# Seven block products in place of eight for 48 of the 160 weight tiles of a hybrid decoder layer

## The chip, the cores and the metric

The kernel runs on one core of one Trainium2 chip. The metric is the device time of one execution in microseconds; the median of three runs is what is compared. The page and the trace come from one further execution, recorded by the hardware profiler.

## The reference, cut to what matters

One layer for 544 tokens (512 of a prompt, 32 of a decode batch) at width 1024, all in fp32:

```python
z = x @ w_in                                     # bg cg hc q k v o ig fg gc gm
conv, new_buf = short_conv(cg * hc, conv_buf, conv_w)
y_conv = (bg * conv) @ w_conv_out
h, C, n, m = mlstm_chunkwise(q, k, v, log i, log f, ...)
y_m = (head_norm(h) * mh_g * sigmoid(o)) @ w_m_out
merged = sigmoid(gc) * y_conv + sigmoid(gm) * y_m
x1 = layer_norm(ALPHA * x + merged @ w_o)
hid = square(relu(x1 @ w_ff1))                   # 4096 wide
x2 = layer_norm(ALPHA * x1 + hid @ w_ff2)
```

The products that the change speaks of are `x` times the columns of gc and gm (both gates), the two branch outputs `w_conv_out` and `w_m_out`, and, of the second MLP product, the parts of two of the four 1024-wide chunks of `hid`.

## The kernel before

Activations lie transposed: 128 partitions, 8 row blocks of the 1024 features, 544 tokens along the free dimension. The weights are 160 tiles of 128 output features each, in the order k, q, o, v, conv (cg, hc, bg for each of 8 feature blocks), w_conv_out, gc, (gm and w_m_out alternating), w_o, and four chunks of 8 first and 8 second MLP tiles.

fp32 accuracy comes from three products of halves. A weight tile is loaded from DRAM (`wload`, L105, SP's queue, 512 KB), ScalarE casts it to a rounded half `wh` (L140) and VectorE takes the rest, `wl = raw - wh` (L141). `mm` (L151) then issues, for each of 8 row blocks, wh times a_h, wh times a_l, wl times a_h, each for two halves of 272 tokens: 48 matmuls to a tile, into one PSUM tile of two banks. The buffers `wr`, `wh`, `wl` are three deep each. Activations are split in the same way (`split`, L555 and L556).

Four PSUM banks serve the products (two tiles of two banks, or four of one where `half`, the loop over one half of the tokens, runs), four more serve everything else (`aux`).

After the gates and k, q, o, v come the prompt's mLSTM and the decode mLSTM, which loads and writes 32 state tiles of 258 KB; the convolution's products run between them. Then, in program order: the convolution output is split into slots 2 and 3, the 8 w_conv_out tiles give y1, the 8 gc tiles give a sigmoid that GpSimd multiplies into y1 (L570), and for each of 8 feature blocks the gm tile, the w_m_out tile and the merge follow, whose result is split again. w_o runs half by half with its weights resident (`resident`, L610 and L611), the first norm of one half beside the other half's products; the MLP's first tiles run the same way, with the resident weights' remainders taken on GpSimd there. Then come whole tiles up to the last 8, which run half by half again beside the second norm.

Every engine's instruction order is fixed before the run: the framework orders them by priority (program order, unless `high_priority` raises a stretch) against its own model of the durations, and a tile takes a buffer of its pool as soon as that model says that one is free. All weight loads go through SP's queue in that order.

Of the kernel before, what the change touches and what calls it, by code (L numbers as in the profile page):

```python
# [31 lines left out]
# columns of the packed small operands  # L32
# [10 lines left out]
# order of the weight tiles  # L43
W_K, W_Q, W_O, W_V, W_CONV, W_YC, W_GC, W_GM, W_OUT, W_FF = 0, 8, 16, 24, 32, 56, 64, 72, 88, 96


@with_exitstack
def tile_hybrid(ctx: ExitStack, tc: tile.TileContext, xT, wt, wg, pk, caug,
# [29 lines left out]
    def slot(i, pl=slots):  # L78
        return pl.tile([P, KT, NT], F32, name=f"slot{i}", tag=f"slot{i}")
# [87 lines left out]
    mstk = ExitStack()          # what the mLSTM keeps to its end  # L167
# [12 lines left out]
    pstk = ExitStack()          # what only the prompt's mLSTM needs  # L180
# [69 lines left out]
    # rows that matmuls spread over the partitions, in exact halves: c, w_inter of the prompt  # L250
# [31 lines left out]
    # per-token columns: a, w_inter, ws, exp(-m)  # L282
# [14 lines left out]
    # decay weights of S, transposed (s on partitions)  # L297
# [17 lines left out]
    qT, so = slot(3), slot(4)  # L315
# [9 lines left out]
    for ft in range(KT):  # L325
        h, d0 = ft // 2, (ft % 2) * P
        ps = mtile(W_V + ft, xh, xl)
        vt = tmp.tile([P, NT], F32, name=f"vt{ft}", tag="cg")
# [5 lines left out]
        vr = tmp.tile([P, 4, NS], F32, name=f"vr{ft}", tag="vr")  # L334
# [118 lines left out]
    # P: rows hi, hi, lo, lo, against v's rows hi, lo, hi, lo  # L453
# [7 lines left out]
    # k*ws: rows hi, hi, lo, lo of the 32 tokens  # L461
# [13 lines left out]
    # q*w_inter, hi and lo, each batch's columns alone  # L475
# [43 lines left out]
    bc = slot(5)  # L519
# [53 lines left out]
    late = pool("late")  # L573
    hh, hl = slot(6, late), slot(7, late)
    for ft in range(KT):
        split(so[:, ft], hh, hl, ft)
    mh, ml = slot(2), slot(3)
    for ft in range(KT):
        ps = mtile(W_GM + 2 * ft, xh, xl)
        sg = tmp.tile([P, NT], F32, name=f"sgm{ft}", tag="cg")  # L580
        nc.scalar.activation(hview(sg), pv(ps), AF.Sigmoid)
        ps = mtile(W_GM + 2 * ft + 1, hh, hl)
        nc.vector.tensor_tensor(hview(sg), pv(ps), hview(sg), op=ALU.mult)
        nc.vector.tensor_tensor(sg, y1[:, ft], sg, op=ALU.add)
        split(sg, mh, ml, ft)

# [33 lines left out]
    def lt(nm, tag, bufs=2, n=HN):  # L620
        return lnp.tile([P, HW], F32, name=nm, tag=tag, bufs=bufs)[:, :n]
# [306 lines left out]
```

## Time and profile before

| what | value |
|---|---|
| median of three runs | 1099.6 us (1097.28 to 1100.43) |
| the profiled execution, first to last instruction | 1099.7 us |
| its mean granted TensorE clock | 0.988 of full speed |
| PE busy (matmul) | 1071.2 us, 97% |
| DVE busy | 535.5 us, 49% |
| ACT busy | 347.9 us, 32% |
| POOL busy | 143.0 us, 13% |
| matmuls | 8351, of them 7680 by L151 |
| moved by DMA | 110.37 MB, 100 GB/s on average |

PE is TensorE's matmul row, PEld its weight loads, DVE VectorE, ACT ScalarE, POOL GpSimd, SP the engine from whose queue most transfers are issued. An engine's busy time says nothing about what it waited for; a duration in the trace holds also the time in which an instruction that had started could not go on.

### The profile page before, as it was taken

How to read it: one execution, taken by the hardware profiler on the slowest of the kernel's cores; microseconds unless marked ns; L12 is line 12 of the kernel's file. 1: busy time of each engine (PE TensorE's matmuls, PEld its weight loads, DVE VectorE, ACT ScalarE, POOL GpSimd, SP SyncE). 2: the span in 40 equal slices, each digit the busy share in tenths (PEclk: the TensorE clock that was granted, in tenths of full speed). 3: DMA queues.
4: the chain of work that ended last, by engine and by line, in shares of the span. 5: the costliest groups of instructions: out<-in, count | busy, mean ns of one | idle time of the engine just before them, and what ended most of it. 6: DMA issues, size and time to landing. Idle time of an engine off the chain costs nothing.

```text
span 1099.7 us, 19420 instructions
## 1 busy us (share of the span) xinstructions
PE 1071.2 (97%) x8351; PEld 1060.0 (96%) x8351; DVE 535.5 (49%) x882; ACT 347.9 (32%) x516; POOL 143.0 (13%) x161
## 2 busy tenths in 40 slices
PE   8999999999999989999999999899999999999994
PEld 8999999999999989999999999899999999999994
DVE  5533223365578778522143359742344234334576
ACT  6431222232234334213222225441233133123432
POOL 1000230000017563003200004200000000000033
PEclk9999999999999999999999999899999999999997
DMA  6222222211136775222222342112222222222201
GB/s 233 98 78 77 97 83 90 77 45 53 40 135 203 241 209 162 95 96 77 97 79 95 123 171 96 58 58 75 80 97 77 97 81 93 94 80 97 96 23 60
DMA packets 34349, 110.37 MB, mean 100 GB/s; under 512 B 3928, under 2 KB 6232, under 8 KB 34008
## 3 DMA queue, kind: packets, MB, share of 16 engines
q1 hardware_dynamic: 31704, 100.69, 28.2%
q0 software_dynamic: 2560, 8.46, 2.0%
q8 instruction: 65, 1.06, 0.4%
q14 instruction: 20, 0.16, 0.1%
HBM read 97.32 MB, written 11.81 MB: 99 GB/s over the span
## 4 chain that ended last, share of the span: by engine, by line
PE 90%; DVE 4%; DMA 3%; ACT 1%; issue 1%; POOL 0%; SPq 0%; DVEq 0%; POOLq 0%; ACTq 0%
PE ps L151 82%; DMA cr<-in_caug_dram 1%; DMA out_cs_dram<-cr 1%; PE u L419 1%; PE pq L496 1%; PE n L405 1%; DVE slot L733 1%; PE S L386 1%; PE n L402 1%; DMA wr<-in_wt_dram 1%; DVE bq L743 1%; DVE slot L671 0%; PE us L507 0%; PE ht L367 0%; PE kt L412 0%
## 5 line engine op out<-in xcount | busy, mean ns | idle before, releaser
L151 PE MATMUL ps<-slot,wh 128*128 128x272 f32 (+1 forms) x4640 | 801.2, 290 | 3.9 <-DVE slot L671 1.8
L151 PEld LDWEIGHTS ps<-slot,wh 128*128 128x128 f32 x4640 | 669.0, 189 | 7.0 <-DVE slot L671 2.5
L151 PE MATMUL ps<-slot,wl 128*128 128x272 f32 (+1 forms) x2320 | 498.2, 289 | 0.0
L151 PEld LDWEIGHTS ps<-slot,wl 128*128 128x128 f32 x2320 | 371.6, 189 | 0.7
L140 ACT CAST wh<-wr 128x1024 fp32r<-128x1024 f32 x145 | 152.1, 1050 | 501.1 <-PE ps L151 437.3
L141 DVE TENSOR_TENSOR wl<-wr,wh 128x1024 fp32r<-128x1024 f32 x142 | 174.1, 1226 | 205.8 <-ACT wh L140 201.7
L151 PE MATMUL ps<-slot,res 128*128 128x272 f32 (+2 forms) x720 | 92.8, 289 | 0.0
L151 PEld LDWEIGHTS ps<-slot,res 128*128 128x128 f32 x720 | 91.3, 188 | 0.3
L726 POOL TENSOR_TENSOR slot<-slot,bc 128x288 f32<-128x288 f32 (+1 forms) x6 | 5.8, 992 | 360.2 <-ACT bc L724 360.2
L810 DVE TENSOR_TENSOR slot<-ps,slot 128x544 f32<-128x544 f32 x16 | 11.6, 725 | 59.3 <-PE ps L151 59.3
L503 POOL TENSOR_SCALAR km<-kk,pkt 128x256 fp32r<-128x256 f32 x32 | 37.3, 1168 | 14.6 <-PE us L507 7.8
L492 ACT CAST ch<-cr 128x516 fp32r<-128x516 f32 x32 | 19.9, 623 | 49.6 <-DMA cr<-in_caug_dram 28.7
L785 ACT CAST slot<-rl 128x544 fp32r<-128x544 f32 (+1 forms) x40 | 22.2, 556 | 37.2 <-DVE rl L784 37.1
L786 DVE TENSOR_TENSOR slot<-rl,slot 128x544 fp32r<-128x544 f32 (+1 forms) x40 | 24.4, 611 | 19.6 <-ACT slot L785 19.4
L509 DVE SCALAR_TENSOR_TENSOR cr<-cr,dec,us 128x258 f32<-128x258 f32 x64 | 29.3, 475 | 3.3 <-PE us L507 3.1
L324 POOL TENSOR_SCALAR slot<-slot,pkt 128x544 f32<-128x544 f32 x8 | 16.8, 2096 | 107.9 <-ACT slot L323 107.9
L493 DVE TENSOR_TENSOR cl<-cr,ch 128x516 fp32r<-128x516 f32 x32 | 22.1, 697 | 17.6 <-ACT ch L492 17.5
L784 DVE TENSOR_TENSOR rl<-rl 128x544 f32<-128x544 f32 (+1 forms) x40 | 24.3, 607 | 11.8 <-ACT rl L783 11.8
L570 POOL TENSOR_TENSOR slot<-slot,sgc 128x544 f32<-128x544 f32 x8 | 14.5, 1809 | 88.1 <-ACT sgc L569 88.1
L783 ACT ACTIVATE rl<-ps 128x544 f32<-128x544 f32 (+1 forms) x40 | 21.2, 529 | 14.3 <-PE ps L151 14.3
L496 PE MATMUL pq<-ch,qm 128*64 128x258 f32 x64 | 18.3, 292 | 5.9 <-ACT wh L140 3.2
L141 POOL TENSOR_TENSOR wl<-wr,wh 128x1024 fp32r<-128x1024 f32 x3 | 7.3, 2423 | 124.9 <-PE am L645 121.2
(258 smaller groups left out, 715.2 us busy)
## 6 DMA issues: line engine op xcount, KB each, us to landing
wr<-in_wt_dram SPq DMA_DIRECT2D x160, 512.0 KB, 3.5
cr<-in_caug_dram SPq DMA_DIRECT2D x32, 258.0 KB, 3.9
out_cs_dram<-cr POOLq DMA_DIRECT2D x32, 258.0 KB, 3.9
slot<-in_xT_dram SPq DMA_DIRECT2D x8, 272.0 KB, 6.3
slot<-in_xT_dram SPq DMA_DIRECT2D x1, 2176.0 KB, 8.5
out_yT_dram<-slot SPq DMA_DIRECT2D x4, 288.0 KB, 2.4
out_cp_dram<-state SPq DMA_DIRECT2D x1, 1028.0 KB
out_yT_dram<-slot SPq DMA_DIRECT2D x4, 256.0 KB, 2.3
```

The costliest lines, as they stand in the source:

```text
L140: nc.scalar.copy(hi, raw)
L141: eng.tensor_tensor(lo, raw, hi.bitcast(F32), op=ALU.subtract)
L151: nc.tensor.matmul(ps[:m, hf, :cs.stop - cs.start], w[:, ws], r(a[:, kt, cs]), start=(kt == 0 and w is wh and a is ah), stop=(kt == KT - 1 ...
L492: nc.scalar.copy(r(chh), cr)
L493: nc.vector.tensor_tensor(r(cl), cr, chh, op=ALU.subtract)
L496: nc.tensor.matmul(pq[:2 * NS, :VW], r(qm[:, dt, bb * 2 * NS:(bb + 1) * 2 * NS]), r(part[:, dt]), start=(bb == 0 and dt == 0 and part is chh),
L503: nc.gpsimd.tensor_scalar(r(km), kk[:, 2 * h:2 * h + 2].rearrange("p a d -> p (a d)"), col("bsel")[:, bb:bb + 1], None, op0=ALU.mult)
L509: nc.vector.scalar_tensor_tensor(cr[:, dt], cr[:, dt], dec[:, h, 4 + bb:5 + bb], pu[:, :VW], op0=ALU.mult, op1=ALU.add)
L783: nc.scalar.activation(view(rl_), src, AF.Relu)
L784: nc.vector.tensor_tensor(rl_, rl_, rl_, op=ALU.mult)
L785: nc.scalar.copy(r(dh[:, ft, cs]), rl_)
L786: nc.vector.tensor_tensor(r(dl[:, ft, cs]), rl_, dh[:, ft, cs], op=ALU.subtract)
```

## The change

Per pair of output feature blocks (j and j+4) the product of a 2 by 2 block weight with a 2 by 2 block activation (feature halves by token halves) is formed from 7 block products in place of 8, in the Winograd form. A block product is 4 row blocks times 3 products of halves, 12 matmuls of 272 columns. A pair has 84 matmuls where two tiles have 96. There are 24 pairs: 4 for gc, 4 for w_conv_out, 4 for gm, 4 for w_m_out, and 4 for each of chunks 1 and 2 of the second MLP product.

```diff
+    class Opset:
+        def sums(self, nm, j, z, eng):
+            t = ztile(f"tt{nm}").rearrange("p a (b n) -> p (a b) n", b=2)
+            x1_ = z[:, 0].rearrange("p (a n) -> p a n", a=2)
+            eng.tensor_tensor(t[:, 0:2], z[:, :, HN:], x1_, op=ALU.subtract)
+            eng.tensor_tensor(t[:, 2], z[:, 1, HN:], t[:, 0], op=ALU.subtract)
+            eng.tensor_tensor(t[:, 3], z[:, 1, :HN], t[:, 2], op=ALU.subtract)
+            split(self.t[0][:, j], self.t[1][:, j], t)
+        def take(self, nm, j, z, eng):
+            ph, pl = self.p
+            split(ph[:, j, 0:2], pl[:, j, 0:2], z[:, :, :HN])
+            split(ph[:, j, 2], pl[:, j, 2], z[:, 1, HN:])
+            self.sums(nm, j, z, eng)
...
+    def halves(nm, src, tag=""):
...
+        nc.scalar.copy(hi, src)
+        nc.vector.tensor_tensor(lo, src, hi.bitcast(F32), op=ALU.subtract)
+    def wpair(i0, i1):
+        a, b = wload(i0), wload(i1)
...
+        a1, a2, b1, b2_ = a[:, :H], a[:, H:], b[:, :H], b[:, H:]
+        tt = nc.gpsimd.tensor_tensor
+        tt(s1, b1, b2_, op=ALU.add)
+        tt(s2, s1, a1, op=ALU.subtract)
+        tt(b1, a1, b1, op=ALU.subtract)
+        tt(s4, a2, s2, op=ALU.subtract)
+        g1 = halves(f"{i0}a", a)
+        g2 = halves(f"{i0}b", s[:, :2 * H])
+        g3 = halves(f"{i0}c", b)
+        g4 = halves(f"{i0}d", s4, "d")
...
+    def spair(i0, i1, X, ev):
+        w = wpair(i0, i1)
+        A = mmt(f"A{nm}")
+        prod(A, w["W11"], X, "X11", True)
+        p1 = ev.part("p1", nm, A[:, :HN])
+        step()
+        F = mmt(f"F{nm}")
+        prod(F, w["W12"], X, "X21", True)
+        ev.add("c11", F[:, :HN], p1)
+        step()
+        prod(A, w["S2"], X, "T2", False)
+        q = ev.part("q", nm, A[:, :HN])
+        D = mmt(f"D{nm}")
+        prod(D, w["S1"], X, "T1", True)
+        prod(A, w["S3"], X, "T3", False)
+        w_ = ev.part("w", nm, A[:, :HN])
+        ev.add("c22", D[:, :HN], w_)
+        def t0():
+            prod(A, w["W22"], X, "T4", False)
+            ev.c21(A[:, :HN])
+        def t1():
+            prod(D, w["S4"], X, "X22", False)
+            ev.add("c12", D[:, :HN], q)
+            ev.done()
+        tail.extend((t0, t1))
...
+    class Evac:
+        def part(self, tag, nm, ps):
+            t = sp.tile([P, HN], F32, name=f"{tag}{nm}", tag=tag, bufs=2 if tag == "q" else 1)
+            nc.scalar.copy(t, ps)
+            return t
+        def add(self, k, ps, t):
+            nc.vector.tensor_tensor(self.block(k), ps, t, op=ALU.add)
+        def c21(self, ps):
+            nc.scalar.copy(self.block("c21"), ps)
...
+    class Added(Evac):
+        def onto(self, k, ps):
+            nc.vector.tensor_tensor(self.block(k), ps, self.block(k), op=ALU.add)
...
+    B = o2set()
+    for j in range(KH):
+        z_ = ztile(f"bz{j}")
+        nc.sync.dma_start(z_, prows(bD, j))
+        B.take(f"b{j}", j, z_, nc.gpsimd)
...
+        def gc(j=j, gz=gz):
+            nc.scalar.activation(gz, gz, AF.Sigmoid)
+            nc.sync.dma_start(prows(cD, j), gz)
+
+        spair(W_GC + j, W_GC + j + KH, X, Evac(gz, gc))
...
+        def gated(j=j, yz=yz):
+            sg = ztile(f"sgc{j}")
+            nc.sync.dma_start(sg, prows(cD, j))
+            nc.vector.tensor_tensor(yz, yz, sg, op=ALU.mult)
+            nc.sync.dma_start(prows(yD, j), yz)
+
+        spair(W_YC + j, W_YC + j + KH, B, Evac(yz, gated))
+    flush()
+    H = o2set()
...
+        def merge(j=j, mz=mz):
+            sg = ztile(f"sgm{j}")
+            nc.sync.dma_start(sg, prows(gD, j))
+            y1 = ztile(f"y1{j}")
+            nc.sync.dma_start(y1, prows(yD, j))
+            nc.vector.tensor_tensor(mz, mz, sg, op=ALU.mult)
+            nc.vector.tensor_tensor(mz, mz, y1, op=ALU.add)
+            split(prows(mh, j), prows(ml, j), mz)
+
+        spair(W_GM + 2 * j + 1, W_GM + 2 * (j + KH) + 1, H, Evac(mz, merge))
+    flush()
...
+    for ck in (1, 2):
+        ahead_()
+        for j in range(1, KH):
+            hidden(ck, j)()
+        ahead_ = hidden(ck + 1, 0)
+        for j in range(KH):
+            i0 = W_FF + 16 * ck + 8
+            spair(i0 + j, i0 + j + KH, D[ck], Added(prows(x1, j)))
+        flush()
```

`wpair` forms four sums of weight halves on GpSimd (512 columns each) and splits seven half tiles (ScalarE casts, VectorE subtracts). `step` runs the two block products that a pair leaves over (t0 and t1) inside the next pair, `flush` runs them at once. One sum of activations, T1 to T4 of a pair of row blocks, is three GpSimd subtractions of 544, 272 and 272 columns. The sums of x are formed during the convolution, whose feature blocks now run in the order 0, 4, 1, 5, 2, 6, 3, 7; for them x is read from DRAM again.

The convolution's result, the mLSTM's, both sigmoids and y1 are written to DRAM (`bD`, `hD`, `cD`, `gD`, `yD`, 2.2 MB each) and read back in pairs of row blocks. After `flush`, the mLSTM's operands H are formed while gm, which takes only x, runs; the convolution's operands B are formed while gc runs. `hidden(ck, j)` makes first MLP tiles j and j+4, and its `put` takes them into the operands of chunk ck. The pools change too: `zz` (three buffers of two row blocks), `sp` (one buffer each of the weight sums `ws`, the outputs `zb`, the last weight half), `o2` (one set of operands). The products of the changed stages use four single banks, `mtile1` replaces `mtile` after the merge, the first chunk's activation takes one buffer `zb` where it had two, the hidden values of chunks 1 to 3 are squared by ScalarE, and `x1` is read in eight transfers in place of one.

## Rows read from the trace of the kernel before

**Rows 1.** Page, part 1: busy time and share of the span by engine.

```profile
PE 1071.2 (97%) x8351; PEld 1060.0 (96%) x8351; DVE 535.5 (49%) x882; ACT 347.9 (32%) x516; POOL 143.0 (13%) x161
```

**Rows 2.** Windows: length, busy us (instructions) by engine, granted clock, DMA share, GB/s.

```profile
215.00:445.00 230.00, 224.14 (x1700) 218.47 (x1699) 162.89 (x369) 79.37 (x131) 67.86 (x94) 0.99 0.42 134
541.00:640.00 99.00, 99.00 (x791) 99.00 (x790) 37.95 (x42) 30.56 (x36) 0.00 (x0) 1.00 0.34 118
640.00:700.00 60.00, 55.72 (x409) 54.22 (x408) 46.87 (x66) 22.20 (x35) 20.00 (x8) 0.94 0.32 106
```

**Rows 3.** Waits: engine and line, releaser, us in total, times, longest.

```profile
ACT wh L140 <- PE ps L151: 437.3, 109, 16.5
```

**Rows 4.** Timeline of the gc stage, VectorE and GpSimd: start, us, instruction.

```profile
498.31 1.36 POOL L570 TENSOR_TENSOR slot<-slot,sgc 128x544 f32<-128x544 f32 x1 [60.10 <-ACT sgc L569]
502.32 1.23 DVE L141 TENSOR_TENSOR wl<-wr,wh 128x1024 fp32r<-128x1024 f32 x1 [4.77 <-ACT wh L140]
502.88 1.88 POOL L570 TENSOR_TENSOR slot<-slot,sgc 128x544 f32<-128x544 f32 x1 [3.21 <-ACT sgc L569]
508.32 1.23 DVE L141 TENSOR_TENSOR wl<-wr,wh 128x1024 fp32r<-128x1024 f32 x1 [4.77 <-ACT wh L140]
```

**Rows 5.** Lines by form: instructions, busy us, mean ns of one, idle before.

```profile
L141 DVE TENSOR_TENSOR wl<-wr,wh 128x1024 fp32r<-128x1024 f32 x142 | 174.1, 1226 | 205.8 <-ACT wh L140 201.7
L556 DVE TENSOR_TENSOR slot<-slot,slot 128x544 fp32r<-128x544 f32 x16 | 10.9, 719 | 0.7 <-ACT slot L555 0.7
L784 DVE TENSOR_TENSOR rl<-rl 128x272 f32<-128x272 f32 x16 | 7.0, 439 | 11.8 <-ACT rl L783 11.8
L689 DVE SCALAR_TENSOR_TENSOR slot<-slot,ps 128x272 f32<-128x272 f32 x16 | 6.8, 432 | 10.5 <-PE ps L151 10.5
L759 POOL TENSOR_TENSOR slot<-slot,bms 128x512 f32<-128x512 f32 x2 | 2.5, 1266 | 7.1 <-ACT bms L756 7.1
L742 POOL TENSOR_TENSOR bs<-bs,slot 128x256 f32<-128x256 f32 x3 | 2.3, 782 | 0.2
L140 ACT CAST wh<-wr 128x1024 fp32r<-128x1024 f32 x145 | 152.1, 1050 | 501.1 <-PE ps L151 437.3
L783 ACT ACTIVATE rl<-ps 128x272 f32<-128x272 f32 x16 | 6.3, 397 | 14.3 <-PE ps L151 14.3
```

**Rows 6.** Timeline of the first norm, VectorE and GpSimd, 662 to 668 us.

```profile
661.98 2.41 POOL L141 TENSOR_TENSOR wl<-wr,wh 128x1024 fp32r<-128x1024 f32 x1 [121.22 <-PE am L645]
662.02 2.62 DVE L648 TENSOR_TENSOR slot<-slot,am 128x544 f32<-128x544 f32 x4 [0.65 <-PE am L645]
665.46 2.40 POOL L141 TENSOR_TENSOR wl<-wr,wh 128x1024 fp32r<-128x1024 f32 x1 [1.07 <-ACT wh L140]
665.65 2.50 DVE L691 TENSOR_TENSOR as<-slot 128x272 f32<-128x272 f32 x1
```

**Rows 7.** Timeline of the same engines where three GpSimd subtractions follow each other.

```profile
685.94 7.71 POOL L611 TENSOR_TENSOR res<-wr,res 128x1024 fp32r<-128x1024 f32 x3 [5.92 <-issue]
686.39 2.54 DVE L671 TENSOR_TENSOR slot<-slot,slot 128x544 fp32r<-128x544 f32 x1 [0.16 <-ACT slot L670]
688.86 2.58 DVE L691 TENSOR_TENSOR as<-as,slot 128x272 f32<-128x272 f32 x1
691.36 2.88 DVE L671 TENSOR_TENSOR slot<-slot,slot 128x544 fp32r<-128x544 f32 x1
```

**Rows 8.** Windows of 3 us over and after that stretch, columns as in rows 2.

```profile
688.00:691.00 3.00, 0.69 (x4) 0.42 (x3) 3.00 (x2) 0.80 (x1) 3.00 (x2) 1.00 0.47 162
691.00:694.00 3.00, 2.19 (x8) 1.73 (x8) 3.00 (x2) 0.00 (x0) 2.66 (x2) 0.66 0.56 184
694.00:697.00 3.00, 2.71 (x12) 2.71 (x13) 3.00 (x6) 1.60 (x3) 0.00 (x0) 0.50 0.51 183
697.00:700.00 3.00, 3.00 (x19) 3.00 (x19) 2.60 (x6) 1.57 (x4) 0.00 (x0) 0.70 0.00 0
```

**Rows 9.** DMA issues between 300 and 430 us: count, KB each, median us to landing.

```profile
wr<-in_wt_dram SPq DMA_DIRECT2D x15, 512.0 KB, 4.3
```

More of the change, by code (lines that the diff above doesn't have):

```diff
@@ L13 @@
 PSUM = bass.MemoryType.PSUM
+DRAM = bass.MemoryType.DRAM
 P = 128
@@ L23 @@
 KT = 8
+KH = KT // 2
 NH = 4
@@ L573, in tile_hybrid @@
[L573 to L585, printed above, removed]
@@ new lines, in prod, with step @@
+    def prod(ps, w, X, which, start):
+        wh, wl = w
+        for kt in range(KH):
+            ws = slice(kt * P, (kt + 1) * P)
+            for n, (w_, lo) in enumerate(((wh, 0), (wh, 1), (wl, 0))):
+                nc.tensor.matmul(ps[:, :HN], w_[:, ws], r(X.get(which, kt, lo)),
+                                 start=(start and kt == 0 and n == 0),
+                                 stop=(kt == KH - 1 and n == 2), skip_group_check=True)
+    tail = []
+    def step():
+        if tail:
+            tail.pop(0)()
@@ L613, in resident, with rplaces @@
         return out
+    def rplaces(t):
+        return sum((spots(slot(k, (P, KT * NT), F32R)) for k in (2, 3)), []) + ppspot(t)
     def half(i, ft, w, ah, al, cs, mid=None):
@@ new lines, in tile_hybrid @@
+    res = resident(W_FF, rplaces(pp), nc.gpsimd)
+    dh, dl = slot(0), slot(1)
+    for hf in range(2):
+        for ft in range(KT):
+            run(ft)
+            ps = half(W_FF + ft, ft, res[ft], xh1, xl1, hv[hf])
+            rl = sp.tile([P, 2, NT], F32, name=f"rl{ft}_{hf}", tag="zb")[:, 0, :HN]
+            nc.scalar.activation(rl, ps, AF.Relu)
+            nc.vector.tensor_tensor(rl, rl, rl, op=ALU.mult)
+            split(dh[:, ft, hv[hf]], dl[:, ft, hv[hf]], rl)
+    ahead_ = hidden(1, 0)
@@ new lines, in tile_hybrid, with sums @@
+    dh, dl = slot(0), slot(1)
+    ahead_()
+    for j in range(1, KH):
+        hidden(3, j)()
+    i0 = W_FF + 56
+    lt2 = Small([o2.tile([P, 15, HW], F32, name="ln2", tag="tl")])
+    res = resident(i0, rplaces(o2.tile([P, 2 * KH * 3 * HN], F32, name="pp2", tag="pp")))
+    for hf in range(2):
+        st = {}
+        def sums(hf=hf, st=st):
+            st["ps"] = aux(f"bm{hf}"), aux(f"bv{hf}")
+            for ps, t0 in zip(st["ps"], (st["s"], st["q"])):
+                nc.tensor.matmul(ps[:, :hv2[hf].stop - hv2[hf].start], onek, t0,
+                                 start=True, stop=False)
+        for ft in range(KT):
+            run(ft)
+            ps = half(i0 + ft, ft, res[ft], dh, dl, hv2[hf], sums if ft == 7 else None)
+            with tc.high_priority(offset=300):
+                norm2_part(lt2, hf, ft, ps, st)
+        if hf == 0:
+            later[1] = lambda st=st: norm2(lt2, 0, st)
+        else:
+            norm2(lt2, 1, st)
```

301 lines of the change are left out of this document (188 added, 113 removed).

## The prediction, on record before the run

> **What bounds the kernel now.** The page's busy shares come first: PE is at work for 1071 of 1099.7 us and no other engine for more than half [rows 1]. The stage windows say where that holds: between 541 and 640 us, in the gm, w_m_out and w_o tiles, PE has not a microsecond free and full clock, while VectorE works 38 of 99 us and GpSimd not at all [rows 2]. The waits agree: ScalarE waits 437 us for PE to give up a weight buffer [rows 3]. So TensorE's instruction stream is the path, and the weights' preparation is hidden. One tile's period is read from the subtraction that splits each: 502.32 to 508.32, 6.00 us [rows 4], for 48 matmuls, 0.125 us each. Fewer matmuls are worth that much, as long as the work per tile elsewhere stays hidden. That is the question, since this change buys 12.5% of TensorE's work in a stage with much more work on VectorE and GpSimd.
>
> **What is removed.** A pair takes 84 x 0.125 = 10.5 us of PE in place of 12.0. Over 24 pairs: 36.0 us, the most that it can give. 16 pairs lie in the gates and branch outputs (192 us now, 168 us of PE after), 8 in the MLP (96 to 84).
>
> **What is added to VectorE and GpSimd.** From the durations by form [rows 5]: a VectorE subtraction of 1024 columns is 1.23 us, of 544 0.72, of 272 0.44; along that slope 512 columns are 0.69 and 1088 are 1.29 (estimates). GpSimd takes 1.27 us for 512, 0.78 for 256, hence some 0.80 for 272, and 1.36 for 544 undisturbed [rows 4].
> - Weights of a pair: four GpSimd sums, 5.1 us, and three and a half VectorE remainders, 3 x 1.23 + 0.69 = 4.4 us (two, 2.5 us, now).
> - Operand sums of one pair of row blocks: GpSimd 1.36 + 2 x 0.80 = 3.0, VectorE 0.72 + 0.44 + 1.29 = 2.5; 5.4 us, 21.6 for the four pairs of B, and again of H.
> - VectorE besides: multiplying by the gate 1.29 for each w_conv_out pair, merge and split 3 x 1.29 = 3.9 for each w_m_out pair, three sums out of PSUM at 0.43 each.
>
> By each engine alone all of this fits under 10.5 us a pair. But do VectorE and GpSimd run at once? A 272-column VectorE add with both inputs in SBUF started at 665.65, took 2.50 us and ended 0.29 us after the GpSimd subtraction that had started at 665.46 [rows 6]; it needs 0.44 otherwise [rows 5]. The other way round, GpSimd's multiply at 502.88 took 1.88 us, and it ended 1.21 us after VectorE's subtraction did [rows 4]. With three GpSimd subtractions in a row, three VectorE adds took 2.54, 2.58 and 2.88 us [rows 7]. VectorE operations that read PSUM are free of this: four at 662.02 took 0.66 us each under a running GpSimd one [rows 6]. So all sums on GpSimd and all remainders on VectorE take turns, and their durations add up. The Trainium skill, "SBUF — State Buffer", section "SBUF: two separate sides", says the same of a VectorE operation with two SBUF inputs against a GpSimd operation that reads SBUF: whichever starts first has the shared port for its whole instruction, and the other is fully blocked. The rows above agree. By that rule alone, without the packing below, the section that follows would be 17 us longer than before.
>
> **The gates and branch outputs.** Taking turns, a pair costs 5.1 + 4.4 = 9.5 us at least. gc with B's sums: 4 x 9.5 + 21.6 = 59 us. w_conv_out: 4 x (9.5 + 1.3) = 43. gm with H's sums: 59, and these can't move: H takes B's buffers, so they lie between the last w_conv_out product and the first of w_m_out. w_m_out: 4 x (9.5 + 3.9) = 54. Together 215 us, against 168 of PE and 192 now. Two corrections. The first pair's 9.5 us are done under the convolution, and the first three w_o remainders (3.7 us) take their place: 209. And an instruction's start overlaps the other engine's end: in rows 7 GpSimd's 3 x 2.41 and VectorE's 0.72 + 0.44 + 0.72, 9.1 us alone, took 8.3 us (685.94 to 694.24), 0.91 of the sum. With that factor: 54 + 42 (here PE) + 54 + 49 - 6 = 193. Rows 7 are two full queues; here a remainder also waits for ScalarE's cast of the sum before it, so I take three quarters of the way from 193 to 209: 205, rounded up to **206, 14 us more than now** (bounds +1 and +17, and above that whatever order leaves idle).
>
> **The clock in these stages.** PE would idle for a fifth of them. After a stretch with 0.69 us of PE work in 3 us the granted clock was 0.66, 0.50 and 0.70 for 9 us [rows 8], which cost (0.34 + 0.50 + 0.30) x 3 = 3.4 us against full clock, the lower level being 1.2 GHz. One such stretch in one of gc and gm that PE can't catch up: **+4** (0 to 10).
>
> **The MLP's 8 pairs.** Turns 9.5 us, PE 10.5: PE still sets the pace. But A is written three times after its first product, and each time VectorE must first have added it to x1 (0.43). Behind a remainder that waits a turn (1.27 + 1.23 = 2.5 us) the add is later than the 1.5 us of products in between, by 1.0 us, at up to three places. I take 1 us a pair: 11.5 against 12.0, **-4** (-12 with none, +8 with two and a half).
>
> **Smaller terms.** Sums of x: 4 x 3.0 us of GpSimd and 4 x 1.29 of VectorE in the decode stretch, where VectorE is at 163 of 230 us, GpSimd at 68 and PE has only 6 us idle [rows 2]: **+2** (0 to 6). Into w_o: after the last product an add, two operations of 1088 and a split, 0.43 + 1.29 + 1.29 + 1.1 + 1.29 = 5.4 us, while w_o's products need row block 3 after 9 matmuls; four banks of nine are 4.5 us, one is 1.1. PE now has no idle there; **+3** (0.9 to 4.3). At nothing: the hidden values' sums, whose chain of some 9 us lies under the next two tiles' 12 us; and the single buffer of the first chunk's activation, 0.40 + 2 x 0.44 + about 0.4 for a cast, 1.7 us in the 3.0 of a half tile; without that cover each would show in full. Traffic through DRAM: 17.8 MB beside 16.8 MB of weights in 206 us, 168 GB/s; at the decode's traffic a load landed after 4.3 us [rows 9], and the next pair's second tile can only be loaded when the last GpSimd sum has freed its buffer: 4.3 + 5.1 = 9.4 us, under 10.5. Nothing (to +8). The output DMAs wait on SP's queue ahead of later weight loads; those waits are inside the same slack.
>
> **Sum.** +14 + 4 - 4 + 2 + 3 = +19 on the profiled 1099.7 us (the median of the runs is 0.1 us lower): **1119 us**. A difference under 0.3%, 3.3 us, is no change that runs of this kernel can tell.
>
> **The rivals.**
> - *TensorE stays the bound (faster).* For this the turns must cost less than rows 6 and 7 show. What speaks for it is that VectorE and GpSimd each fit alone; against it are six rows. The point of decision: 4 pairs with their operand sums under 42 us, so 42 / 59 = 0.71 of the added durations, where rows 7 gave 0.91. Time: 1099.7 - 36 + 3 + 2, and 0.3 us lost per pair at PSUM: 1076 us (1064 to 1086). Chance 0.17.
> - *The turns dovetail.* The section at +2, the MLP at -8, the rest +4: 1098 us (1086 to 1105). Chance 0.15, of it 0.06 faster, 0.05 no change, 0.04 slower.
> - *The lower clock holds.* If PE's gaps in gc, gm and w_m_out keep it at 1.2 GHz for 20 us of each, these become PE-bound again at twice the price: some 10 us for each, 30 us in place of 4: 1145 us and more (to 1170). Rows 8 show 9 us of it after a single gap; against it, PE recovered there. Chance 0.08.
> - *The forecast*, 1105 to 1145 us: 0.60.
>
> So faster 0.17 + 0.06 = 0.23, no change 0.05, slower 0.60 + 0.08 + 0.04 = 0.72. The range 1086 to 1150 leaves out the first rival and about half of the third. The forecast's own is 1105 to 1145.
>
> **What would show it.** The matmuls of the tiles fall from 7680 to 7392 (24 x 12 fewer). In gc and gm VectorE's remainders last well over their 1.23 us and GpSimd's sums over 1.27, with PE's idle ended by VectorE or by a cast behind it; gm lasts near 55 us where 8 tiles take 48. The MLP's pairs last 10.5 to 12 us. If remainders keep 1.23 us beside running sums, or gm lasts 42 us, the step on turns is wrong and the first rival holds. If PE's idle is ended by DMA, the loads are what I have mispriced.

## The result and the profile after

The changed kernel takes 1129.7 us (median of four runs, 1127.49 to 1131.15) where the kernel before, measured beside it, takes 1099.96: a ratio of 1.027, 95% interval 1.0253 to 1.0287. It is slower by 30 us. Its profiled execution has a span of 1127.7 us at a mean granted clock of 0.978. Two single executions further down, one of e6's ten (1156.8 us) and one of e11's four (1139.7 us), ran at a mean granted clock of 0.84 and are left out of those medians. The engines' busy time, from the page, against [rows 1]:

```profile
PE 1055.6 (94%) x8063; PEld 1034.1 (92%) x8063; DVE 663.5 (59%) x1008; ACT 438.2 (39%) x676; POOL 356.3 (32%) x309
```

The 288 matmuls that the change saves are gone (8351 to 8063). VectorE is busy 128 us longer and GpSimd 213 us longer; that includes the time in which an instruction that had started was held.

Where the 28 us of span lie is read by stages. A stage ends here with its last product matmul, counted in the trace: 1536 end the v and head stage, 1152 more the convolution with the decode, then 336 for each seven-product stage (384 for eight), 384 for w_o, 384 for the first MLP tiles (by count: some of w_o's first products run among w_m_out's last). Windows between these ends (length, busy us and instructions by engine in the order PE, PEld, VectorE, ScalarE, GpSimd, granted clock, DMA share, GB/s), first of before: the four gate and branch stages together, w_o, the first MLP tiles, the rest of the MLP but its last 384 products.

```profile
441.10:633.50 192.40, 192.40 (x1539) 192.40 (x1538) 64.55 (x71) 49.56 (x58) 14.47 (x8) 1.00 0.29 95
633.50:682.60 49.10, 49.10 (x391) 48.94 (x390) 34.48 (x50) 17.91 (x24) 12.29 (x5) 1.00 0.41 138
682.60:740.00 57.40, 53.12 (x391) 51.70 (x389) 39.11 (x68) 28.94 (x62) 7.71 (x3) 0.94 0.17 57
740.00:1029.50 289.50, 288.95 (x2307) 288.74 (x2306) 108.35 (x120) 78.38 (x97) 0.00 (x0) 1.00 0.27 87
```

The same view of after: convolution and decode, then gc, w_conv_out, gm, w_m_out, w_o, the first MLP tiles, the MLP.

```profile
212.80:447.90 235.10, 227.34 (x1687) 218.61 (x1687) 166.06 (x358) 77.04 (x122) 89.96 (x113) 0.97 0.48 158
447.90:505.50 57.60, 45.59 (x338) 43.24 (x338) 41.22 (x42) 31.54 (x47) 37.98 (x26) 0.99 0.45 155
505.50:552.60 47.10, 44.21 (x337) 43.32 (x337) 24.83 (x30) 20.55 (x32) 20.85 (x16) 0.98 0.49 168
552.60:612.50 59.90, 47.65 (x339) 45.68 (x338) 44.01 (x41) 31.21 (x49) 44.99 (x29) 0.94 0.49 164
612.50:666.70 54.20, 46.63 (x338) 45.13 (x337) 38.95 (x40) 25.24 (x37) 21.14 (x12) 0.94 0.52 161
666.70:725.60 58.90, 52.45 (x391) 51.32 (x390) 38.24 (x55) 18.69 (x29) 12.65 (x5) 0.94 0.39 133
725.60:778.90 53.30, 50.02 (x391) 49.17 (x390) 37.48 (x70) 29.65 (x65) 7.76 (x3) 1.00 0.20 63
778.90:1057.50 278.60, 277.62 (x2211) 276.91 (x2210) 143.19 (x165) 109.45 (x151) 80.19 (x56) 1.00 0.28 90
```

Before, PE was busy for all 192.4 us of the four stages. After, they take 218.8 us and PE works 184.1 of them: +26.4 us. Convolution and decode cost 6.7 us (228.4 before), w_o 9.7. The MLP gives back 10.9 and its first tiles 4.1; the last products and the tail are +1.2 and -1.2. That makes +27.8 of the 28.0.

What the two engines do in the four stages, as lines by form (count, busy us, mean ns of one, idle before). GpSimd's 512-column sum took 1266 ns alone [rows 5]:

```profile
L656 POOL TENSOR_TENSOR ws<-wr,ws 128x512 f32<-128x512 f32 x15 | 26.2, 1745 | 0.0
L653 POOL TENSOR_TENSOR ws<-wr 128x512 f32<-128x512 f32 x15 | 24.5, 1631 | 74.6 <-DMA wr<-in_wt_dram 10.6 <-DVE wl75d L643 10.2 <-DVE wl56d L643 9.0
L654 POOL TENSOR_TENSOR ws<-ws,wr 128x512 f32<-128x512 f32 x15 | 23.2, 1547 | 1.0
L655 POOL TENSOR_TENSOR wr<-wr,wr 128x512 f32<-128x512 f32 x15 | 20.4, 1360 | 0.0
L643 DVE TENSOR_TENSOR wl66a<-wr,wh66a 128x1024 fp32r<-128x1024 f32 x1 | 2.4, 2394 | 0.0
L550 DVE TENSOR_TENSOR pp<-bz,pp 128x544 fp32r<-128x544 f32 x4 | 6.2, 1540 | 0.6 <-ACT pp L549 0.6
L550 DVE TENSOR_TENSOR tl<-tth,th 128x1088 fp32r<-128x1088 f32 x4 | 5.1, 1286 | 1.9 <-ACT th L549 1.9
```

A pair's four weight sums are 1745 + 1631 + 1547 + 1360 ns, 6.28 us, of GpSimd, not the 5.1 of an undisturbed engine, and B's 544-column remainder takes 1540 ns for 720. Of the 46 weight remainders of 1024 columns in these stages 16 take more than 1.3 us, the longest 2.39 (wl66a); the others keep their 1.23. H's 1088-column remainder is not stretched.

A second thing shows in the timeline of two pairs of gc (chosen rows: start, us, instruction, idle time before it and what ended it):

```profile
481.05 0.44 DVE L730 TENSOR_TENSOR gz<-F,p 128x272 f32<-128x272 f32 x1 [3.46 <-DMA cD<-gz]
485.46 0.43 DVE L730 TENSOR_TENSOR gz<-D,q 128x272 f32<-128x272 f32 x1
485.99 1.11 ACT L769 ACTIVATE gz<-gz 128x1088 f32<-128x1088 f32 x1 [0.57 <-DVE gz L730]
487.12 0.57 SPq L770 DMA_DIRECT2D cD<-gz  x1
487.58 1.28 POOL L653 TENSOR_TENSOR ws<-wr 128x512 f32<-128x512 f32 x1 [6.38 <-DMA wr<-in_wt_dram]
490.25 1.05 ACT L642 CAST wh67b<-ws 128x1024 fp32r<-128x1024 f32 x1 [2.88 <-POOL ws L654]
490.38 0.44 DVE L730 TENSOR_TENSOR gz<-F,p 128x272 f32<-128x272 f32 x1 [3.89 <-DMA cD<-gz]
491.33 1.23 DVE L643 TENSOR_TENSOR wl67b<-ws,wh67b 128x1024 fp32r<-128x1024 f32 x1 [0.51 <-ACT wh67b L642]
491.43 2.28 POOL L656 TENSOR_TENSOR ws<-wr,ws 128x512 f32<-128x512 f32 x1
```

A pair's last block is added at 485.46, the sigmoid follows, and the write to DRAM is issued at 487.12. Only at 490.38 may the next pair's first block be added, since `zb` is one buffer and is free when that write has landed. VectorE stands idle for 3.89 us. In this pair that costs PE next to nothing; one pair earlier the same add had waited 3.46 us, and PE then stood 1.71 us for the PSUM bank that the add empties. The remainder wl67b, which comes next, was not held by the add: it starts when its cast ends (490.25 + 1.05), the cast waited for GpSimd's sum, and GpSimd had waited 6.38 us for the pair's weights. So the loading of weights is a third candidate. The last two rows show the turns once more: GpSimd's sum starts 0.10 us into wl67b, takes 2.28 us for 1.27, and ends 1.15 us after it. The waits of the four stages list these (chosen lines: us in total, times, longest):

```profile
DVE gz L730 <- DMA cD<-gz: 12.3, 3, 5.0
POOL ws L653 <- DMA wr<-in_wt_dram: 10.6, 3, 6.4
DVE yz L730 <- DMA yD<-yz: 10.0, 3, 3.8
DVE mm L730 <- DMA gD<-mz: 5.1, 1, 5.1
DVE mz L730 <- DMA gD<-mz: 4.2, 2, 3.6
PE F L670 <- DVE gz L730: 3.5, 2, 1.8
```

So there are two theories of the 26 us: **turns** (GpSimd's sums and VectorE's remainders, as the prediction had it), and **the output buffer** (one `zb` and its trip to DRAM, which the prediction put at nothing). A third stands beside them: **the chain that prepares a pair's weights** (load, sums, cast, remainder, one after the other).

### The profile page after: what moved, and what is told of

Same layout as the page of the kernel before. It is cut to its first block, busy times and chain, and to the rows that moved or that the text cites. A ratio compares the mean times of both kernels' runs of the same rounds, so it can differ in the third digit from the quotient of the medians.

```text
span 1127.7 us, 19561 instructions
## 1 busy us (share of the span) xinstructions
PE 1055.6 (94%) x8063; PEld 1034.1 (92%) x8063; DVE 663.5 (59%) x1008; ACT 438.2 (39%) x676; POOL 356.3 (32%) x309
## 4 chain that ended last, share of the span: by engine, by line
PE 29%; POOL 9%; DVE 7%; DMA 6%; issue 5%; ACT 3%; DVEq 0%; POOLq 0%; SPq 0%; ACTq 0%
PE ps L1053 14%; PE ps L177 8%; DMA wr<-in_wt_dram 4%; PE A L670 3%; PE D L670 2%; POOL ws L654 2%; POOL ws L656 2%; POOL ws L653 1%; PE F L670 1%; DMA gD<-mz 1%; POOL wr L655 1%; DVE x L979 1%; DVE x L915 1%; DMA cD<-gz 1%; POOL tth L571 1%
## 5 line engine op out<-in xcount | busy, mean ns | idle before, releaser
L177 PE MATMUL ps<-slot,wh 128*128 128x272 f32 (+2 forms) x1984 | 357.4, 294 | 4.8 <-ACT slot L549 3.6
L177 PEld LDWEIGHTS ps<-slot,wh 128*128 128x128 f32 x1984 | 292.3, 191 | 8.2 <-ACT slot L549 4.3
L177 PE MATMUL ps<-slot,wl 128*128 128x272 f32 (+2 forms) x992 | 219.5, 292 | 0.0
L177 PEld LDWEIGHTS ps<-slot,wl 128*128 128x128 f32 x992 | 161.9, 191 | 0.5
L1053 PE MATMUL ps<-xh,wh 128*128 128x272 f32 x384 | 82.5, 288 | 0.0
L1053 PE MATMUL ps<-xh,wl 128*128 128x272 f32 x384 | 82.4, 288 | 0.0
L1053 PE MATMUL ps<-pp,wh 128*128 128x272 f32 x384 | 82.4, 288 | 0.0
L1053 PEld LDWEIGHTS ps<-xh,wh 128*128 128x128 f32 x384 | 61.6, 188 | 0.0
L1053 PEld LDWEIGHTS ps<-pp,wh 128*128 128x128 f32 x384 | 61.6, 188 | 0.0
L1053 PEld LDWEIGHTS ps<-xh,wl 128*128 128x128 f32 x384 | 61.1, 189 | 0.0
L177 PE MATMUL ps<-slot,slot 128*128 128x272 f32 (+2 forms) x384 | 50.9, 290 | 2.5 <-DVE mm L730 2.5
```

The source lines that it names most:

```text
L177: nc.tensor.matmul(ps[:m, hf, :cs.stop - cs.start], w[:, ws], r(a[:, kt, cs]), start=(kt == 0 and w is wh and a is ah), stop=(kt == KT - 1 ...
L1053: nc.tensor.matmul(pss[hf], w[:, ws], r(a[:, kt, cs]), start=(kt == 0 and n == 0), stop=(kt == KT - 1 and n == 2))
```

## The experiments

Times are medians, ratios are to the kernel before, measured beside each. The stages are read from one profile each, as above, in us, and can differ by 0.2 from the rounded windows; "four" is gc to w_m_out together.

| kernel | total | ratio (95%) | conv, decode | gc | w_conv_out | gm | w_m_out | four | w_o | MLP |
|---|---|---|---|---|---|---|---|---|---|---|
| before | 1099.0 to 1101.4 | 1 | 228.4 | | | | | 192.4 | 49.1 | 289.5 |
| after | 1129.7 | 1.027 (1.0253 to 1.0287) | 235.1 | 57.6 | 47.1 | 59.9 | 54.3 | 218.8 | 58.8 | 278.6 |
| e1 all sums on VectorE | 1108.1 | 1.0072 (1.0047 to 1.0097) | 238.4 | 52.5 | 45.3 | 49.2 | 49.5 | 196.5 | 57.4 | 276.7 |
| e2 no weight sums | 1117.2 (one run) | | 240.6 | 55.9 | 47.8 | 54.0 | 47.2 | 204.8 | 55.5 | 276.8 |
| e3 two output buffers | 1120.5 | 1.0193 (1.0170 to 1.0217) | 240.5 | 51.5 | 42.6 | 57.5 | 48.4 | 200.1 | 59.2 | 278.5 |
| e4 two weight-sum buffers | 1127.1 | 1.0267 (1.0236 to 1.0297) | 233.3 | 61.6 | 47.1 | 57.9 | 50.2 | 216.9 | 57.4 | 276.8 |
| e5 plain branch outputs | 1095.5 | 0.9966 (0.9951 to 0.9982) | 234.7 | 49.0 | 48.1 | 47.6 | 48.1 | 192.7 | 50.9 | 278.4 |
| e6 MLP alone | 1096.0 | 0.9967 (0.9948 to 0.9985) | 232.6 | 49.2 | 48.1 | 48.1 | 48.1 | 193.6 | 51.1 | 278.6 |
| e7 = e1 + e3 | 1091.5 | 0.9930 (0.9906 to 0.9955) | 234.6 | 51.6 | 42.2 | 50.1 | 42.3 | 186.2 | 58.6 | 276.5 |
| e8 = e2 + e3 | 1091.1 (one run) | | 234.0 | 50.5 | 42.6 | 46.8 | 43.3 | 183.1 | 56.2 | 276.5 |
| e9 = e5 + e7 | 1083.1 | 0.9847 (0.9798 to 0.9896) | 233.0 | 44.5 | 48.1 | 43.0 | 48.1 | 183.8 | 50.9 | 276.5 |
| e10 = e9, bD from GpSimd | 1084.8 | 0.9855 (0.9822 to 0.9887) | 229.6 | 44.8 | 48.1 | 43.2 | 48.1 | 184.2 | 50.9 | 276.5 |
| e11 = e7, merge by halves | 1089.5 | 0.9892 (0.9849 to 0.9935) | 235.2 | 53.2 | 42.2 | 48.8 | 42.2 | 186.4 | 52.3 | 276.5 |
| e12 weight sums on VectorE | 1111.8 | 1.0106 (1.0064 to 1.0148) | 234.6 | 55.7 | 45.5 | 54.4 | 47.4 | 203.1 | 58.3 | 276.7 |

One stage of one profile is not exact: the convolution has the same instructions in the same order in after, e3 and e4 and shows 235.1, 240.5 and 233.3 us. A difference of a few us in that stage therefore shows nothing by itself.

**e1, all sums on VectorE.**

```diff
-                X.sums(f"x{j}", j, z_, nc.gpsimd)
+                X.sums(f"x{j}", j, z_, nc.vector)
...
-        tt = nc.gpsimd.tensor_tensor
+        tt = nc.vector.tensor_tensor
...
```

The sums of B, H and the MLP's chunks move in the same way.

> All sums of weights and activations move from GpSimd to VectorE; nothing else changes. Theory 1 (GpSimd's sums and VectorE's two-input operations take turns, and this sets the pace of the gates and branch outputs): nothing waits for a turn any more, and a 512-column sum costs 0.69 us on VectorE in place of 1.27 on GpSimd. VectorE then has 4 x (4.4 + 2.8 + 1.3) + 16 = 50 us in gc and in gm, 42 in w_conv_out (TensorE's own), 49 in w_m_out: some 191 us for the stretch that took 218.8, and 1095 to 1108 us in all. Theory 2 (the one buffer of outputs and its trip through DRAM sets the pace): no change, 1124 to 1132 us. Theory 3 (the loads and the chain of preparing weights set it): shorter sums shorten that chain by 2 us a pair, but VectorE's queue is fuller: 1115 to 1130 us.

21.6 us of the 30 are gone and the four stages are 22.3 us shorter: the place of the sums is worth most of it, as the turns theory had it (the total is at that theory's upper bound, the stages 5.5 us above its 191). The page of e1, and three of its lines by form in 447 to 635 us:

```profile
PE 1048.8 (95%) x8063; PEld 1030.7 (93%) x8063; DVE 692.8 (63%) x1164; ACT 437.7 (40%) x676; POOL 130.2 (12%) x153
```

```profile
L653 DVE TENSOR_TENSOR ws<-wr 128x512 f32<-128x512 f32 x15 | 10.3, 686 | 0.3 <-DMA wr<-in_wt_dram 0.2
L656 DVE TENSOR_TENSOR ws<-wr,ws 128x512 f32<-128x512 f32 x15 | 10.2, 683 | 0.0
L550 DVE TENSOR_TENSOR pp<-bz,pp 128x544 fp32r<-128x544 f32 x4 | 2.9, 720 | 2.8 <-ACT pp L549 2.8
```

A sum takes 0.69 us on VectorE, where GpSimd took 1.36 to 1.75. GpSimd is 226 us less busy and VectorE only 29 us more: its own operations are no longer stretched, as B's remainder shows, 720 ns for 1540, and none of the 46 weight remainders takes over 1.23 us.

**e2, weight sums left out.**

```diff
-        tt(s1, b1, b2_, op=ALU.add)
-        tt(s2, s1, a1, op=ALU.subtract)
-        tt(b1, a1, b1, op=ALU.subtract)
-        tt(s4, a2, s2, op=ALU.subtract)
...
```

The weight halves `b` and `a2` are split in place of the sums, so the outputs are not the reference's.

> The four GpSimd sums of each pair's weights are left out (raw weight halves stand in their place, so the products are others); loads, casts, remainders, products and operand sums stay. Theory 1: turns fall by 5.1 us a pair, to 39 us in gc and gm and 33 in w_m_out, all under TensorE's 42: the stretch of the gates and branch outputs falls from 218.8 to 170 to 182 us, the total to 1080 to 1093 us. Theory 2 (one buffer of outputs and its trip through DRAM): the stretch stays over 205 us, 1114 us or more. Theory 3 (loads and the preparation chain): the chain loses its sums, so it falls as in theory 1, unless the loads themselves are late; then 1105 us or more.

A miss for the turns alone: without any weight sum the four stages still take 204.8 us (one run). Something else paces them too; by this run it can be the output buffer or late loads.

**e3, two output buffers.**

```diff
-        return pl.tile([P, 2, NT], F32, name=name, tag=tag)
+        return pl.tile([P, 2, NT], F32, name=name, tag=tag, bufs=2 if tag == "zb" else 3)
...
```

The first chunk's activation gets its second buffer back with it; the first MLP tiles take 53.3 us with and without.

> The outputs of a pair get two buffers in place of one, so that a pair's first sums need not wait until the last pair's outputs have left for DRAM. Theory 1: the turns stay; at most the waits of VectorE for those transfers (some 27 us in the trace, in a stretch where it waits for turns anyway) shift: 1122 to 1132 us. Theory 2 (this buffer and its trip set the pace): 15 to 25 us less, 1105 to 1115 us.

The four stages lose 18.7 us with every sum where it was, and w_conv_out runs at PE's own pace in this window of e3:

```profile
505.30:547.90 42.60, 42.43 (x338) 42.20 (x337) 26.36 (x31) 20.32 (x32) 23.78 (x17) 1.00 0.58 191
```

The total moves by only 9.2 us, to 1120.5, between the two cases of the expectation. The profiled convolution is 5.4 us longer, but the three executions without a profile were no faster (1119.2 to 1122.7 us against 1118.7), so where the rest of the 18.7 went is not shown. The output buffer is a cause as well. The turns are as they were: the 46 weight remainders average 1.46 us as in after. The largest entry among GpSimd's waits in the four stages is now the third candidate (10.6 us in after):

```profile
POOL ws L653 <- DMA wr<-in_wt_dram: 19.5, 4, 5.6
```

**e4, two buffers of weight sums.** This asks whether GpSimd's long waits for the last remainder of the pair before (up to 10.2 us each in its row above) are the pace.

```diff
-        s = sp.tile([P, 3 * H], F32, name=f"ws{i0}", tag="ws")
+        s = sp.tile([P, 3 * H], F32, name=f"ws{i0}", tag="ws", bufs=2)
```

> The weight sums get two buffers in place of one, so that GpSimd can form the next pair's sums before the last remainder of this pair is taken (GpSimd waits for that remainder for some 60 us in the trace). Theory 1: the sum of turns is the same, they only come earlier: 1120 to 1131 us. Theory 3 (the chain of preparing weights, held up by its single buffer, sets the pace): 10 to 25 us less, 1105 to 1118 us.

They aren't: 1127.1 us, an interval that overlaps that of after. GpSimd's waits there were those of an engine that had time. This holds beside one output buffer; a second `ws` together with a second `zb`, or more buffers for the weight loads, were not tried.

**e12, only the weight sums on VectorE** (the edit of `tt` in e1's diff).

> The changed kernel with one edit: the four sums of each weight pair on VectorE, the sums of operands left on GpSimd, one buffer of outputs. If the operand sums on GpSimd are worth the 8 us by which the gate stages stood higher without weight sums (55.9 and 54.0) than with all sums on VectorE (52.5 and 49.2): gc and gm 54 to 57, yc and mout 45 to 50, section 202 to 207, total 1112 to 1118. If moving the weight sums alone gives it all: section 196 to 198, total 1105 to 1110. If weight sums on VectorE cost more than leaving them out: section above 208, total above 1119.

1111.8 us, 0.2 below the first case's bounds, its stages inside them. It fits e2: moving the weight sums to VectorE is worth as much as leaving them out (203.1 and 204.8 us). What e1 has beyond e12 in the stages is in gc and gm, where B's and H's sums lie: 55.7 to 52.5 and 54.4 to 49.2, with w_m_out 2.1 longer. In the time the two intervals overlap.

**e7, both cures; e8, both without weight sums.**

> All seven-product stages, every sum on VectorE and two buffers of outputs. If the two causes are separate and add: the 21.6 us of the first and the 9 us of the second, 1097 to 1101, gates section 178 to 186. If they are two views of one wait: no gain over sums on VectorE alone, 1106 to 1109, gates section 195 to 198.

> The four sums of each weight pair left out (halves of the raw weights stand in their place, so the outputs are not the reference's) and two buffers of outputs. If weight sums and the single output buffer are the only paces: gates section 172 to 180 us (TensorE's own 168 plus filling), total 1085 to 1095. If operand sums and in-order queues pace as well: gates section 190 to 200, total 1105 to 1113.

Neither cure contains the other: the second buffer is worth 0.77% alone and 1.42% where the sums are on VectorE already, the sums' place 1.98% alone and 2.63% beside two buffers. e7 is 0.7% faster than the kernel before, and its total is 5.5 us under the first case's bounds; its four stages, 186.2, are at that case's upper bound. Times and stages disagree on how the two add up: both together give 3.40%, more than 1.98 + 0.77, but 32.6 us of the four stages, less than 22.3 + 18.7. The convolution differs by 3.8 and 5.9 us between e7's profile and those of e1 and e3, so nothing is shown either way. (e7's profile is of its slowest execution of five, 1095.5 us.) In its windows of w_conv_out and w_m_out PE never stops, and VectorE carries remainders and sums in 34 and 39 of 42 us. Before each of them stands a gate stage (gc, gm) with the operand sums of B or H:

```profile
448.40:500.00 51.60, 46.54 (x338) 45.16 (x337) 43.97 (x66) 31.19 (x47) 0.00 (x0) 0.93 0.58 200
500.00:542.20 42.20, 42.20 (x338) 42.20 (x337) 34.42 (x48) 21.30 (x33) 0.00 (x0) 1.00 0.57 190
542.20:592.30 50.10, 46.12 (x338) 44.98 (x337) 46.91 (x69) 30.54 (x48) 0.00 (x0) 0.93 0.61 199
592.30:634.60 42.30, 42.30 (x339) 42.22 (x338) 38.51 (x49) 24.32 (x36) 0.00 (x0) 1.00 0.58 185
```

In the branch outputs that is the eighth of PE's time which the change was to buy. The gate stages keep 51.6 and 50.1 us, near the 50 of VectorE's work that e1's expectation had counted there; VectorE was busy 44.0 and 46.9 of them, and what paces them is not shown further. e8's time is e7's (1091.1, one run, and 1091.5), but it differs from e7 in two things, no weight sums and operand sums on GpSimd, so what the weight sums still cost is not shown. Its total is in the first case, but its four stages came at 183.1, between the two cases of its expectation: gc and gm stay at 50.5 and 46.8, with B's and H's sums still on GpSimd.

**e5, plain branch outputs; e6, seven products in the MLP alone.** In e5:

```diff
...
-        spair(W_YC + j, W_YC + j + KH, B, Evac(yz, gated))
...
+        for a in range(2):
+            ps = mtile1(W_YC + j + KH * a, bh, bl)
+            for hf in range(2):
+                nc.vector.tensor_tensor(yz[:, a, hv[hf]], ps[hf], sg[:, a, hv[hf]], op=ALU.mult)
...
```

The same for w_m_out; the operand sums of B and H go. e6 does it for gc and gm too and drops x's sums.

> Both gates and the MLP pairs stay by seven products; the two branch outputs go back to eight plain block products, so the operand sums of B and H are gone, while x's sums and all trips through DRAM stay. Turns theory (GpSimd and VectorE sums set the pace): gates section 180 to 192 us (two plain stages at 48, two gate stages at 42 to 48), entry into w_o back to 49 to 51, total 1083 to 1098. Output-buffer theory (one buffer of outputs and its trip set the pace): gc and gm stay at 51 to 57 each, section 200 to 208, total 1104 to 1114.

> Seven products only in the MLP's two chunks: all gates and branch outputs by eight plain products, x's sums gone, the trips through DRAM kept in the new order. If the trips cost nothing and x's sums are what made the conv and decode stage longer: conv back to 228 to 229, gates section 192 to 194, w_o 49, MLP's second products 11 us less than before, total 1085 to 1091. If the trips through DRAM themselves cost: conv stays at 235 and gates at 198 or more, total 1096 to 1106.

e5 has the total of the turns theory (1095.5), but its four stages, 192.7, lie just above that theory's bounds: gate pairs by seven products with the sums on GpSimd and one output buffer gain nothing over plain ones (49.0 and 47.6). e6's total (1096.0) is at the edge of its second case; its four stages (193.6) are in the first, and its convolution (232.6) lies between the two, nearer to the second. By stage: the MLP gave 10.9 and the first MLP tiles 4.1, but without x's sums the convolution kept 4.2 of the 6.7 (less apart than the same code's 233.3 and 240.5), w_o kept 2.0 and the last products cost 2.8 (55.0 for 52.2).

**e9, gates and MLP with both cures; e10, the writes of bD moved.** e9 is e5 with the edits of e1 and e3. e10 is e9 with

```diff
-        nc.sync.dma_start(bD[:, ft], bc)
+        nc.gpsimd.dma_start(bD[:, ft], bc)
```

> Gates and MLP pairs by seven products, branch outputs by eight, every sum on VectorE, two buffers of outputs. If the sums' place and the single output buffer are all that kept the two gate stages at 49.0 and 47.6 us: 42 to 45 each, gates section 181 to 186, total 1082 to 1088. If the gate stages are held by something else (queues in order, the operand sums of x): 47 to 49 each, total 1092 to 1096.

> The kernel of the run before it in this call, with the eight writes of the branch input to DRAM issued from GpSimd's queue in place of SyncE's, where the decode loads stand behind them. If the place in SyncE's queue is what makes conv and decode longer: 234 down to 228 to 231, total 3 to 6 us less than its sibling. If it is the traffic itself or x's sums: conv 233 to 236, total within 2 us of its sibling, or slower where GpSimd, which waits for each written tile, delays the decode's masks.

Both gate stages come near PE's own 42 us when both cures are in and the operand sums of B and H are out. e9 lies in its first case and has the lowest median of the kernels here, 0.9847 of before. Its gc, gm and w_o windows:

```profile
445.40:489.90 44.50, 43.47 (x338) 42.44 (x337) 33.81 (x46) 27.24 (x38) 0.00 (x0) 1.00 0.63 219
538.00:581.00 43.00, 42.53 (x338) 42.31 (x337) 31.91 (x42) 26.46 (x37) 0.00 (x0) 1.00 0.64 218
629.20:680.00 50.80, 49.36 (x390) 48.99 (x389) 35.56 (x55) 18.26 (x28) 12.60 (x5) 1.00 0.47 156
```

e10's convolution is 3.4 us shorter, inside its first case, but the total is 1.7 us higher, with intervals that overlap: inconclusive. If the place in SyncE's queue costs something, it is too little to show in the time.

**e11, the last merge by halves.** The entry into w_o. In after PE waits twice there (waits of PE, 660 to 700 us):

```profile
PE ps L177 <- ACT slot L549: 3.5, 2, 2.5
PE ps L177 <- DVE mm L730: 2.5, 1, 2.5
```

The last branch pair's c12 block comes with its very last product, and the merge waits for all four blocks. VectorE's order adds to it:

```profile
670.23 1.05 ACT L844 CAST slot<-wr 128x1024 fp32r<-128x1024 f32 x1 [1.63 <-DMA wr<-in_wt_dram]
671.31 1.23 DVE L845 TENSOR_TENSOR slot<-wr,slot 128x1024 fp32r<-128x1024 f32 x1 [1.45 <-ACT slot L844]
672.45 0.43 DVE L730 TENSOR_TENSOR mm<-D,q 128x272 f32<-128x272 f32 x1
```

The last product ended at 669.3, but its add begins only at 672.45: a remainder of w_o's weights stands in front of it, whose cast had waited for its load. The first of the two waits is of this order. Windows of 3 us from there show what follows:

```profile
673.00:676.00 3.00, 1.33 (x9) 1.11 (x9) 2.51 (x2) 0.37 (x1) 0.00 (x0) 0.83 0.93 334
676.00:679.00 3.00, 2.17 (x8) 1.85 (x9) 1.29 (x1) 2.97 (x4) 0.00 (x0) 0.50 0.95 389
679.00:682.00 3.00, 3.00 (x15) 3.00 (x15) 2.67 (x3) 1.03 (x2) 0.00 (x0) 0.53 0.24 53
682.00:685.00 3.00, 3.00 (x26) 3.00 (x25) 1.00 (x3) 0.00 (x0) 0.00 (x0) 1.00 0.77 277
```

The granted clock falls to its lower level, 1.2 GHz, for some 6 us. e11 is e7 with the merge cut in two: the left columns, which the first eight w_o tiles read, are merged when c21 is there, one product earlier, and those tiles take the last pair's rows last. The loads of the gate and of y1 for the merge are also issued before the pair's products (in after the last of them was issued at 660.97 and landed 4.05 us later, before the merge began, so they were not what it waited for).

```diff
...
+            nc.scalar.copy(self.block("c21"), ps)
+            if self.left:
+                self.left()
...
-            ps = half(W_OUT + ft, ft, res[ft], mh, ml, hv[hf])
+            ps = half(W_OUT + ft, ft, res[ft], mh, ml, hv[hf], ks=(0, 1, 2, 4, 5, 6, 3, 7))
...
```

> All seven-product stages, every sum on VectorE, two buffers of outputs, and the last branch output merged by column halves: the left half, which the first eight tiles of the next stage read, once its block is there and before the last product, and those tiles take the rows of the last pair last. If the late merge of the last pair is what made the entry into w_o long: 58.6 down to 50 to 53, total 1083 to 1087. If it is something else (the loads of x, weights kept resident): 57 to 59, total 1090 to 1093.

w_o takes 52.3 us for 58.6, at full clock:

```profile
634.20:686.50 52.30, 49.78 (x390) 48.96 (x389) 40.19 (x62) 20.63 (x32) 12.68 (x5) 1.00 0.52 172
```

In e7 PE waited there once, 4.5 us, for the same cast (L549); in e11 that wait is gone. So the late merge is the cause of most of this term; how much of it is the merge itself and how much the order in VectorE's queue is not parted. The total, 1089.5, is above the expected range and its interval overlaps e7's: in these profiles gc, the first MLP tiles and the convolution took 3.6 us of the gain back, which is not separated from chance here.

## Why the prediction was right or wrong

The direction, the range and the place were right: 1119 forecast in 1086 to 1150, 1129.7 measured, and the four gate and branch stages hold nearly all of it. The first rival (PE stays the bound), the dovetailing turns and the lower clock held through are out. The total is closer than its parts, and that is luck: against the forecast's terms the four stages with their clock are 8.4 us too long, w_o 6.7 and the convolution 4.7, while the MLP's second products are 6.9 and its first tiles 4.1 too short.

- **Turns.** Shown in the rows after: GpSimd's sums at 1.36 to 1.75 us, 16 of 46 weight remainders stretched, and GpSimd held from 0.10 us into wl67b until its end. The Trainium skill, "SBUF — State Buffer", section "SBUF: two separate sides", calls this an exclusive lock for the whole instruction. The 2.28 us for 1.27 agree. By e12 (weight sums) and e1 (all sums) their place is worth 18 and 21.6 us. The runs don't part the lock from GpSimd's plain slowness, though: VectorE needs half the time for the same sum (0.69 against 1.27 us alone).
- **The step that was mis-sized is the correction of the turns and, with it, the output buffer at nothing.** The plain sum of turns, 215 us, was cut to 206 for packing. Measured were 218.8. By stage the plain sum was 59, 43, 59, 54 and the trace has 57.6, 47.1, 59.9, 54.3. But that agreement is partly an accident: the plain sum contains no wait for `zb`, and e3, which leaves all turns in place, brings the four stages to 200.1, below the corrected 206. With two buffers the turns cost less than forecast, and the DRAM trip behind one buffer, which I had put "inside the same slack", costs 18.7 us of these stages in one profile (9.2 in the time). The sentence looked at queues and traffic and left out what holds the buffer: 1.1 us of sigmoid and 3.2 us of write before the next pair may begin.
- **Clock, +4.** The four windows show 0.99, 0.98, 0.94 and 0.94, so 8.4 us at most by estimate, had PE been the bound throughout (0.01 x 57.6 + 0.02 x 47.1 + 0.06 x 59.9 + 0.06 x 54.2). That is inside the bounds; no run separates its price.
- **MLP, -4.** Mis-sized: -10.9, PE busy 277.6 of 278.6 us. The late adds of 1 us a pair did not happen; the bound "-12 with none" was nearest.
- **x's sums, +2.** The stage is 6.7 us longer. e6, without these sums, still has 4.2, but the 2.5 between them is less than the same code varies (233.3 to 240.5), so neither the sums' part nor the rest is separated; e10 points to the place of bD's writes without settling it.
- **Into w_o, +3.** Mis-sized: +9.7, above the bound of 4.3. The chain was listed, and PE needed its first four links, 4.1 us in the list (0.43 + 1.29 + 1.29 + 1.1). They took 7.5 (669.3 to 676.78), because the add at their head stands behind a w_o remainder. PE had 2.5 us of products under them and waited 5.0. The lower clock after the gap was not in the sum: PE's busy time in w_o is 52.45 us for 49.10. e11 takes back 6.3 of it, and plain branch outputs (e5) 7.9.
- **Not foreseen:** the first MLP tiles are 4.1 us shorter. In after their window has full clock and in before 0.94, the dip of [rows 8]. Why the gap is smaller was not tried.
- **Signs announced.** Matmuls: right. Remainders "well over their 1.23 us": 16 of 46, and GpSimd's sums on average. PE's idle "ended by DMA" if the loads are mispriced: PE's never was directly; VectorE's was, by writes, and GpSimd's, by weight loads (10.6 us).

## What to carry to other kernels

Work that saves TensorE time must be paid by engines that run beside each other: where both read SBUF as here, take the sum of their durations as a price on the high side for sums on GpSimd and remainders on VectorE (215 us by that sum; 200.1 once the output buffer was doubled), and see first whether one engine alone does both in less (here VectorE did, with 29 us more for 226 us less). For each output that leaves through DRAM ask what holds its buffer until the write has landed, and which engine waits for the add that waits for the buffer; the list of waits names both, but GpSimd's long waits on it (e4) were worth nothing. Where two tiles are made as one pair of four blocks, the last pair's blocks come late together: order the next stage so that it doesn't begin with them, or leave the pairs out there, as e9 does. A gain read from one stage of one profile counts only where the time shows it too: e3's 18.7 us of stages were 9.2 in the time.

## What the hardware showed that was not expected

- Taking all sums, 226 us of busy time, from GpSimd made VectorE, which got all of it, only 29 us busier (663.5 to 692.8 us). The Trainium skill, "GPSIMD Engine Reference", section "4.1 Engine selection", puts elementwise work on VectorE and has GpSimd some 2 times slower with two inputs. The runs come near it: alone it was 1.27 against 0.69 us here, 1.85 times, and beside VectorE up to 2.6 times (1.75 against 0.68).
- After 5 us of PE waits between 670 and 677 us the granted clock was 0.50 and 0.53 for 6 us, also while PE was busy throughout (679 to 682), and 1.00 from there.
